# Transposing the values of a linear attention through VectorE squares and device memory

## The chip, the cores and the metric

The kernel runs on one core of a Trainium2 chip. The core has a TensorE (PE in the profile) that multiplies matrices and writes its sums to PSUM, a VectorE (DVE), a ScalarE (ACT), a GpSimd (POOL) and a SyncE (SP), each with an instruction queue of its own that is worked off in order. DMA engines move data between device memory and the on-chip memory SBUF; here SP issues nearly all transfers. The metric is the device time of one execution in microseconds (us), lower is better.

## The reference: what is computed

Two layers of an encoder over 16 learned meta tokens and 256 grid tokens (272 positions, width 2048), in float32. Each layer projects the residual stream `h` once and splits the columns:

```
proj = jnp.einsum('bld,dp->blp', h, w_in)
gq, gk, gv, gr, glr, nq, nk, nv = jnp.split(proj, points, axis=-1)
y_gla = _gla_mixer(gq, gk, gv, gr, glr, gla_w_up, gla_b_up, gla_norm_w)
y_na = _na_mixer(nq, nk, nv, na_rel_bias)
mix = jnp.einsum('blm,md->bld', jnp.concatenate([y_gla, y_na], axis=-1), w_out)
h = _layer_norm(DEEPNORM_ALPHA * h + mix, ln1_w, ln1_b)
ff = square(relu(h @ w_ff1)) @ w_ff2
h = _layer_norm(DEEPNORM_ALPHA * h + ff, ln2_w, ln2_b)
```

The change touches `gv`, the values of the gated linear attention: 4 heads of 256 columns. In that attention a position's output is a sum over positions of scores times values, `einsum('bhts,bhse->bhte', scores, vi)`, so the values are needed with positions as rows. The neighbourhood attention (`_na_mixer`) and the squared-ReLU MLP fill the rest of the layer.

## The kernel before

**Layout.** Activations lie transposed: features on the 128 partitions, positions along the free axis. `x` is 16 tiles of 128 x 272. Every float32 operand is held as two parts, a rounded high part and the rest (`split`, L337-339: an ACT copy and a DVE subtract), and a product is three matmuls: high by high, low by high, high by low.

**Weights.** `weights` and `made` (L180-198) stream the weights in pieces of 128 x 1024 (512 KB): SP loads `raw` (L194), ACT rounds it to `wh` (L217), DVE subtracts to `wl` (L218). Each of the three has three buffers. So a piece's `wh` can be written once PE is done with the piece three before it, and PE then has two more pieces to work on before it needs the new one. A full piece is 24 matmuls of 272 columns (`eight`, L252); where 256 columns are wanted, it is 8 of 512 and 8 of 256.

**Order of the work.** `by_m` walks over output tiles of 128 columns (two pieces each) and calls `pump` between pieces. `pump` takes steps from two queues of Python generators, `fg` and `bg`, which hold the side work: the decay gates (`gates`, L452), the transposes of the values (`v_rows`, L508), the attention heads. A `yield True` marks that the next step contains PE work, and pump spaces such steps. The code is then ordered per engine by a scheduler; what each engine runs is a fixed list.

**The place of the change.** Early in each layer the values are projected, tile by tile, each evicted by `ev_v` (L501): ACT copies the 128 x 272 sum from PSUM to `ft` (L503). Two tiles make one head, and `v_rows` turns a head's two tiles: six TensorE transposes against an identity matrix (L516) into two PSUM banks, then per tile a `split` (L518) of the 256 grid positions into `V` and `vlow` (tiles named `y`), and a `stack` (L519) of the 16 meta positions into `VS`: two ACT copies (L344) and a DVE subtract (L345). `V`, `vlow` and `VS` are read much later, by L715-719 in `gla_head`.

Around it, `gates` multiplies all `x` tiles by a thin matrix (L468), copies the result (`lrt`, L473), builds `lr`, and per head issues two small matmuls (L486), then on ACT two absolute values (L487), an exponential (L488), a logarithm (L489) and a last exponential (`dec`, L492), with a DVE step (L491) between. The next pieces' `wh` copies stand in the same ACT queue.

Of the kernel before, what the change touches and what calls it, by code (L numbers as in the profile page):

```python
# [7 lines left out]
F32 = mybir.dt.float32  # L8
# [6 lines left out]
P = 128  # L15
D = 2048
DC = D // P
T = 256
NM = 16
L = T + NM  # L20
DEPTH = 2
ROWS, GW = 4, 64
GH, GDK, GDV = 4, 128, 256
# [14 lines left out]
MEET = 2  # L38
PAD = 40
PITCH = 288  # L40
WIDE = 1280
HIGHS = {"once": (0, P, 2 * P), "two": (0, P, 2 * P), "all": (0, P, 2 * P), "all2": (0, P, 2 * P), "own2": (0, P + 48, 2 * P + 64)}
LOWS = {"once": (16, P + 32, 2 * P + 64), "two": (16, P + 16, 2 * P + 64), "all": (0, P + 16, 2 * P + 64),
# [15 lines left out]
class Trunk:  # L59
    def __init__(self, ctx, tc, ins, out):  # L60
        self.ctx, self.tc, self.nc = ctx, tc, tc.nc
        self.i, self.out = ins, out
        self.bg, self.fg, self.credit, self.fcredit = deque(), deque(), 0, 0
        self.wants, self.due, self.late, self.low = {}, None, 0, True
        self.x = [None] * DC
        self.stream, self.ready = self.order(), deque()
        pool = lambda name, **k: ctx.enter_context(tc.tile_pool(name=name, **k))
        self.cp = pool("const", bufs=1)
        self.xp = pool("xhl", bufs=1)
        self.yp = pool("yhl", bufs=1)  # L70
        self.wp = pool("wst", bufs=3)
        self.jp = pool("jn", bufs=1)
        self.pm = pool("pm", bufs=4, space=PSUM)
        self.pb = pool("pb", bufs=4, space=PSUM)

    def bank(self):
        return self.pb.tile([P, 512], F32, name="bg", tag="bg")
# [108 lines left out]
    def made(self, ap, ends, kind):  # L186
# [3 lines left out]
        raw = self.wp.tile([P, WB], F32, name="raw", tag="raw")  # L190
        wh, wl = (self.wp.tile([P, WIDE], F32R, name=nm, tag=nm) for nm in ("wh", "wl"))
        wh, wl = self.blocks(wh, *HIGHS[kind]), self.blocks(wl, *LOWS[kind])
# [154 lines left out]
    def pair(self, pool, name, c):  # L347
        both = pool.tile([P, 2, PITCH], F32R, name=f"{name}{c}", tag=f"{name}{c}", bufs=1)
        return Pair(both, dense=name in ("y", "u") and not self.full)


    def layer(self, l):
        nc, tc = self.nc, self.tc
        self.l = l
        self.full = l + 1 < DEPTH
        self.n = n = L if self.full else T
        with ExitStack() as actx:
            pool = lambda name, side, ctx=actx, bufs=1: ctx.enter_context(
                tc.tile_pool(name=name, bufs=bufs, side=side, reuse_waits="tile"))
            a = pool("att", "left")  # L360
            t = lambda nm, s: a.tile(s, F32, name=nm, tag=nm)
            self.qk = [t(f"qk{h}", [P, 2, L]) for h in range(GH)]
            for h in range(GH) if l else ():
                nc.gpsimd.memset(self.qk[h][:, 1, T:], 0.0)
            self.decay = [t(f"dec{h}", [P, 2, L]) for h in range(GH)]
            self.V = a.tile([P, 2 * GH, 2, P], F32R, name="V", tag="V")
            self.vlow = [self.pair(self.yp, "y", 12 + h).both.rearrange("p a c -> p (a c)") for h in range(GH)]
            self.VS = a.tile([80, GH * GDV], F32R, name="VS", tag="VS")
            nc.gpsimd.memset(self.VS.bitcast(F32), 0.0)
            self.y, self.gate, self.done, self.vt = [None] * DC, {}, set(), []  # L370
            if l:
                self.load_gates()
                self.by_m(self.x, [L + 2] * 4, lambda m, ps: self.fixed(self.ev_k, m, ps), pump=(1, NORMS[0]),
                          renew=True)
                first = self.by_k(self.x, L, self.normed)
                self.drain()
                self.lctx.close()
            with ExitStack() as ectx:
                self.ep = pool("early", "right", ectx)
                self.fcredit = 0  # L380
                self.fg.append(self.gates())
                if l == 0:
                    with ExitStack() as xctx:
                        self.xr = pool("xr", "right", xctx)
                        first = self.by_k(self.x, L, self.load_x, wide=True)
                    for m in range(4):
                        self.ev_k(m, first.pop(0)[0])
                for m, ps in enumerate(first):
                    self.ev_v(m, ps[0])
                self.credit, self.alone = 0, True  # L390
                self.by_m(self.x, [L] * 4, lambda m, ps: self.ev_v(4 + m, ps), pump=(1, 1, True))
                self.by_m(self.x, [n] * 4, self.ev_q, pump=(1, 1, True))
                self.drain()
            self.a2 = pool("na", "left", bufs=2)
            with ExitStack() as gctx:
                self.credit = 0
                self.g2 = pool("gla", "right", gctx, 2)
                for h in range(GH):
                    self.bg.append(self.gla_head(h))
                for g in range(2):  # L400
                    self.by_m(self.x, [n] * 4, lambda m, ps: self.ev_r(4 * g + m, ps), pump=(1, GLA_R))
                self.na_tiles()
                for g in range(6):
                    if g == 5:
                        while self.bg:
                            self.step(self.bg, 1)
                        gctx.close()
                        self.ln_open()
                    ns = [n if (4 * g + m) % 3 == 0 else L for m in range(4)]
                    self.by_m(self.x, ns, lambda m, ps: self.ev_na(4 * g + m, ps), pump=(1, GLA_NA, True))  # L410
            self.alone = False
            ps = self.by_k(self.y, n, self.mixed)
            self.drain()
        self.tail(ps)
# [29 lines left out]
    def load_gates(self):  # L444

        place = lambda c: self.yp.tile([P, 2, PITCH], F32, name=f"gw{c}", tag=f"y{c}", bufs=1).rearrange("p a c -> p (a c)")[:, :512]
        *self.wup, self.wlr = (place(c) for c in (8, 9, 10))
# [51 lines left out]
        self.nc.scalar.activation(self.qk[m][:, 0, :], ps, AF.Identity, **how)  # L499

    def ev_v(self, c, ps):  # L501
        vt = self.ep.tile([P, L], F32, name="ft", tag="ft", bufs=4)
        self.nc.scalar.copy(vt, ps)  # L503
        self.vt.append(vt)
        if c % 2:
            (self.fg if c > 3 else self.bg).append(self.v_rows(c // 2, self.vt[-2:]))

    def v_rows(self, h, vt):  # L508

        nc = self.nc  # L510
        yield True
        pt = self.spare(2)
        for i in range(3):
            n = P if i < 2 else NM
            for e in range(2):
                nc.tensor.transpose(pt[e][:n, i * P:i * P + P], vt[e][:, i * P:i * P + n], self.ident)  # L516
        for e in range(2):
            self.split(pt[e][:, :T], self.V[:, 2 * h + e].rearrange("p i c -> p (i c)"), self.vlow[h][:, e * T:e * T + T])  # L518
            self.stack(pt[e][:NM, T:T + P], self.VS[:, h * GDV + e * P:h * GDV + e * P + P], NM, (0, 32), 64)  # L519
            yield  # L520

    def ev_na(self, j, ps):
# [504 lines left out]
    def reuse(self, name, c, dtype):  # L1027

        t = self.xp.tile([P, 2, PITCH], dtype, name=f"{name}{c}", tag=f"x{c}", bufs=1)
        return t.rearrange("p a c -> p (a c)")[:, :512]  # L1030
# [237 lines left out]
```

## Time and profile before

| what | value |
|---|---|
| median of 3 runs | 2325.73 us (2324.75 to 2325.81) |
| the profiled execution | 2325.9 us, of which the span from first to last instruction is 2324.1 us |
| PE / ACT / DVE / POOL busy | 2311.4 / 1230.7 / 1527.8 / 130.1 us |
| granted TensorE clock, mean | 0.999 |
| weight pieces | 770 groups of `wh` copies (805.0 us of ACT) and as many `wl` subtracts (937.8 us of DVE) |
| transposes of values (L516) | 48 matmuls, from 62.8 us to 1283.6 us |

The busy share is an average over the span. A row of a timeline gives start, length, engine, line, operation, tiles and count; in square brackets stands how long the engine was idle before it and what ended that. A matmul's length is longer than its distance to the next one, since matmuls are pipelined, so what a piece costs is read from the starts. ACT's rows also overlap by about 0.1 us.

### The profile page before, as it was taken

Reading aid. Unit: us, or ns where it says so; the run is one execution under the profiler, and the core shown is the slowest. Engines: PE = TensorE matmul, PEld = TensorE weight load, DVE = VectorE, ACT = ScalarE, POOL = GpSimd, SP = SyncE. Lnnn points to the kernel's source line nnn. Section 1 sums busy time; section 2 is a strip of 40 time slices with the busy share of each in tenths; the row PEclk is TensorE's granted clock in tenths of the full one; section 3 lists DMA queues with packets and bytes.
Section 4 is the critical chain, followed back from the end, with each engine's and each line's share of the span. In section 5 each row is a group of like instructions: output and inputs, shape, how many; then the busy total and the mean of one; then the engine's idle time right before and its main releaser. Section 6 shows DMA issues by size and latency. Waiting matters only on the chain.

```text
span 2324.1 us, 45342 instructions
## 1 busy us (share of the span) xinstructions
PE 2311.4 (99%) x18516; PEld 2197.5 (95%) x18516; DVE 1527.8 (66%) x2440; ACT 1230.7 (53%) x2128; POOL 130.1 (6%) x200
## 2 busy tenths in 40 slices
PE   9999999999999999999999999999999999999999
PEld 9999999999999999999999899989988888888888
DVE  5588777775544455547576788878866545666655
ACT  5666765564433344444456767655655334555443
POOL 0021110110000000000020021100100000000000
PEclk9999999999999999999999999999999999999999
DMA  8455545555555555555655555555666666667664
GB/s 265 154 164 153 155 149 167 173 181 181 181 179 178 180 181 182 179 179 178 182 183 166 175 170 160 155 172 181 197 193 193 192 196 192 191 198 221 191 195 150
DMA packets 118304, 419.07 MB, mean 180 GB/s; under 512 B 13512, under 2 KB 14024, under 8 KB 118096
## 3 DMA queue, kind: packets, MB, share of 16 engines
q1 hardware_dynamic: 117808, 415.65, 57.9%
q8 instruction: 145, 2.38, 0.4%
q14 instruction: 63, 0.52, 0.1%
q10 hardware_dynamic: 288, 0.52, 0.1%
HBM read 414.03 MB, written 2.10 MB: 179 GB/s over the span
## 4 chain that ended last, share of the span: by engine, by line
PE 96%; DVE 2%; ACT 1%; issue 1%; DMA 0%; POOL 0%; DVEq 0%; ACTq 0%; SPq 0%; POOLq 0%
PE mm L252 56%; PE mm L264 30%; PE mm L303 4%; PE mm L313 2%; PE bg L303 1%; DVE wl L218 1%; PE bg L837 0%; PE bg L627 0%; PE bg L468 0%; PE mm L775 0%; ACT wh L217 0%; DVE acc L1071 0%; PE mm L801 0%; PE bg L969 0%; PE mm L516 0%
## 5 line engine op out<-in xcount | busy, mean ns | idle before, releaser
L218 DVE TENSOR_TENSOR wl<-raw,wh 128x1024 fp32r<-128x1024 f32 (+1 forms) x770 | 937.8, 1225 | 633.9 <-ACT wh L217 531.5
L217 ACT CAST wh<-raw 128x1024 fp32r<-128x1024 f32 (+1 forms) x770 | 805.0, 1047 | 764.5 <-PE mm L252 344.3
L252 PE MATMUL mm<-x,wh 128*128 128x272 f32 (+3 forms) x4544 | 805.8, 294 | 0.0
L252 PEld LDWEIGHTS mm<-x,wh 128*128 128x128 f32 x4544 | 646.9, 188 | 15.7 <-issue 0.8
L252 PE MATMUL mm<-x,wl 128*128 128x272 f32 (+3 forms) x2432 | 519.8, 284 | 0.0
L252 PEld LDWEIGHTS mm<-x,wl 128*128 128x128 f32 x2432 | 390.7, 188 | 0.0
L252 PE MATMUL mm<-y,wh 128*128 128x272 f32 (+1 forms) x1440 | 235.0, 285 | 0.0
L252 PEld LDWEIGHTS mm<-y,wh 128*128 128x128 f32 x1440 | 199.8, 188 | 0.1
L264 PE MATMUL mm<-x,wh 128*128 128x512 f32 x832 | 193.8, 390 | 0.0
L264 PEld LDWEIGHTS mm<-x,wh 128*128 128x128 f32 x832 | 154.3, 188 | 31.0
L252 PE MATMUL mm<-u,wh 128*128 128x272 f32 (+1 forms) x1056 | 172.1, 285 | 0.0
L264 PE MATMUL mm<-y,wh 128*128 128x512 f32 x688 | 162.3, 389 | 0.0
L264 PEld LDWEIGHTS mm<-y,wh 128*128 128x128 f32 x688 | 128.6, 188 | 26.9 <-issue 0.4
L252 PE MATMUL mm<-y,wl 128*128 128x272 f32 (+1 forms) x720 | 146.4, 284 | 0.0
L252 PEld LDWEIGHTS mm<-u,wh 128*128 128x128 f32 x1056 | 146.3, 188 | 0.0
L264 PE MATMUL mm<-u,wh 128*128 128x512 f32 x496 | 118.2, 390 | 0.0
L252 PEld LDWEIGHTS mm<-y,wl 128*128 128x128 f32 x720 | 112.6, 188 | 0.0
L264 PEld LDWEIGHTS mm<-u,wh 128*128 128x128 f32 x496 | 90.9, 188 | 17.6
L252 PE MATMUL mm<-u,wl 128*128 128x272 f32 (+1 forms) x528 | 107.3, 284 | 0.0
L264 PEld LDWEIGHTS mm<-x,wl 128*128 128x128 f32 x832 | 98.4, 188 | 2.0
L264 PE MATMUL mm<-x,wl 128*128 128x256 f32 x832 | 98.8, 276 | 0.0
L264 PEld LDWEIGHTS mm<-y,wl 128*128 128x128 f32 x688 | 84.3, 188 | 2.8
(288 smaller groups left out, 2301.6 us busy)
## 6 DMA issues: line engine op xcount, KB each, us to landing
raw<-in_wff SPq DMA_DIRECT2D x512, 512.0 KB, 3.6
raw<-in_win SPq DMA_DIRECT2D x190, 512.0 KB, 3.8
raw<-in_wout SPq DMA_DIRECT2D x64, 512.0 KB, 3.7
nb<-in_nab SPq DMA_DIRECT2D x16, 352.0 KB, 4.3
xraw<-in_xT SPq DMA_DIRECT2D x7, 272.0 KB, 5.7
out<-out SPq DMA_DIRECT2D x5, 256.0 KB, 3.0
brow<-in_norm SPq DMA_DIRECT2D x4, 256.0 KB, 4.8
gw<-in_wup SPq DMA_DIRECT2D x4, 196.0 KB
```

Of the source, the lines that this page charges most:

```text
L217: self.nc.scalar.copy(h, r)
L218: self.wl = self.nc.vector.tensor_tensor(lo, r, h.bitcast(F32), ALU.subtract).ins
L252: mm(o, lhsT=self.block(w, j), rhs=rhs, start=first and not i, stop=last and i == len(TURNS[once]) - 1)
L264: self.nc.tensor.matmul(o, lhsT=self.block(both[j // 8][low], j % 8), rhs=rhs, start=first and not i + j, stop=bool(last and i and j == 15 ...
L303: self.nc.tensor.matmul(ps[g + m][:, :n], lhsT=self.block(parts[p][0], 4 * j + m if first else 2 * m + j), rhs=acts[k + j][parts[p][1]][:, ...
L313: self.nc.tensor.matmul(o, lhsT=self.block(both[low], i), rhs=rhs, start=not low and k + i % 2 == 0, stop=k == DC - 2 and i % 2 == 1 and n ...
```

## The change

`ev_v` now pads each 128 x 272 tile with 16 zero columns (a GpSimd memset) to 288, and DVE transposes it in 32 x 32 squares into half of a tile `vt`; each square is turned in place, so the four 32-row bands of a tile still have to be brought side by side. `v_rows` does that with transfers on ACT's queue: it writes a head's `vt` (128 x 576) to a buffer in device memory, `vhop`, and reads it back in nine pieces, eight of 32 partitions x 4 x 64 into `vr` and one of 16 x 4 x 64 into `vm`. `split` and `stack` then read those from SBUF. The TensorE transposes and their two PSUM banks go; the generator has four steps in place of three, and the first is not marked as PE work. Per head that is two DVE transposes, two memsets and ten DMAs more and six matmuls less, eight times in the program.

```diff
+        self.hp = pool("hop", bufs=2, space=bass.MemoryType.DRAM)
...
     def ev_v(self, c, ps):
-        vt = self.ep.tile([P, L], F32, name="ft", tag="ft", bufs=4)
-        self.nc.scalar.copy(vt, ps)
-        self.vt.append(vt)
-        if c % 2:
-            (self.fg if c > 3 else self.bg).append(self.v_rows(c // 2, self.vt[-2:]))
+        h, e = divmod(c, 2)
+        vt = self.ep.tile([P, VR * 32], F32, name="ft", tag="ft", bufs=2)
+        if not e:
+            self.vt = self.ep.tile([P, VR, 2, 32], F32, name="vt", tag="vt", bufs=3)
+        self.nc.scalar.copy(vt[:, :L], ps)
+        self.nc.gpsimd.memset(vt[:, L:], 0.0)
+        self.nc.vector.transpose(self.vt[:, :, e, :], vt)
+        if e:
+            (self.fg if c > 3 else self.bg).append(self.v_rows(h, self.vt))
...
     def v_rows(self, h, vt):
-        nc = self.nc
-        yield True
-        pt = self.spare(2)
-        for i in range(3):
-            n = P if i < 2 else NM
-            for e in range(2):
-                nc.tensor.transpose(pt[e][:n, i * P:i * P + P], vt[e][:, i * P:i * P + n], self.ident)
+        nc, e = self.nc, self.ep
+        hop = self.hp.tile([P, VR, 64], F32, name="vhop", tag="vhop")
+        nc.scalar.dma_start(hop, vt.rearrange("p j e c -> p j (e c)"))
+        yield
+        rows, meta = e.tile([P, 2, 4, 64], F32, name="vr", tag="vr", bufs=2), e.tile([NM, 4, 64], F32, name="vm", tag="vm", bufs=2)
+        at = hop.rearrange("(a k) j c -> k j a c", a=4)
+        for j in range(VR - 1):
+            nc.scalar.dma_start(rows[j % 4 * 32:j % 4 * 32 + 32, j // 4], at[:, j])
+        nc.scalar.dma_start(meta, at[:NM, VR - 1])
+        yield
         for e in range(2):
-            self.split(pt[e][:, :T], ...)
-            self.stack(pt[e][:NM, T:T + P], ...)
+            src = rows[:, :, :, 32 * e:32 * e + 32]
+            self.split(src, ...)
+            self.stack(meta[:, :, 32 * e:32 * e + 32], ...)
             yield
```

In the lists below a row gives the line, the operation, output and inputs with their numbers, and the shape; `x5` is five in a row. Lines of the changed kernel are two later up to `gates` and twelve later from `silu` on, so L219 is the `wh` copy and L220 the `wl` subtract.

**PE, first layer, behind the gates' thin matmuls (`ws`).** Before, head 0's six transposes stand ahead of the next piece:

```order
L468 MATMUL bg_802<-x15_623,ws_765 64x272
L516 MATMUL mm_849<-ident_635,ft_726 128x128
L516 MATMUL mm_850<-ident_635,ft_728 128x128
L516 MATMUL mm_849<-ident_635,ft_726 128x128
L516 MATMUL mm_850<-ident_635,ft_728 128x128
L516 MATMUL mm_849<-ident_635,ft_726 16x128
L516 MATMUL mm_850<-ident_635,ft_728 16x128
L252 MATMUL mm_862<-x0_130,wh_769 128x272 x2
```

After, the piece follows the thin matmuls at once:

```order
L470 MATMUL bg_819<-x15_625,ws_777 64x272
L254 MATMUL mm_877<-x0_132,wh_783 128x272 x2
L254 MATMUL mm_877<-x1_133,wh_783 128x272 x2
L254 MATMUL mm_877<-x0_132,wl_784 128x272
L254 MATMUL mm_877<-x1_133,wl_784 128x272
```

The same is so at the other seven heads; nothing takes the transposes' place on PE.

**ACT, first layer, from the copies of the first values to the gates' `lrt`.** Before, three pieces are rounded there (769, 864, 911):

```order
L503 COPY ft_730<-bg_107 128x272
L217 CAST wh_769<-raw_768 128x1024
L503 COPY ft_732<-bg_108 128x272
L217 CAST wh_864<-raw_863 128x1024
L217 CAST wh_911<-raw_910 128x1024
L473 COPY lrt_835<-bg_802 32x272
```

After, one (783) is; heads 0 and 1 are sent off, and head 0's read-back waits for its write to land:

```order
L518 DMA vhop_780<-vt_729 128x576
L508 COPY ft_742<-bg_110 128x272
L219 CAST wh_783<-raw_782 128x1024
L518 DMA vhop_1019<-vt_738 128x576
L523 DMA vr_866<-vhop_780 32x4x64 x5
L508 COPY ft_812<-mm_746 128x272
L523 DMA vr_866<-vhop_780 32x4x64 x3
L524 DMA vm_867<-vhop_780 16x4x64
L475 COPY lrt_852<-bg_819 32x272
L219 CAST wh_879<-raw_878 128x1024
```

The second and third pieces (879, 926, which answer to 864 and 911) have moved behind `lrt`.

**ACT, first layer, the gates of heads 1 to 3 (`gt`, `dec`).** Before, piece 1061 is rounded ahead of them:

```order
L217 CAST wh_1061<-raw_1060 128x1024
L492 ACTIVATE dec1_85<-gt_944 128x544
L488 ACTIVATE gt_987<-gt_987 128x544
L338 CAST V_88<-mm_997 128x256
L489 ACTIVATE gt_987<-gt_987,one_659 128x544
L344 CAST VS_93<-mm_997 16x128 x2
L503 COPY ft_1040<-mm_954 128x272
```

After, the piece that answers to it, 1081, comes behind all of them and behind head 1's read-back, of which this is the end:

```order
L489 ACTIVATE gt_1058<-bg_1056 128x272
L489 ACTIVATE gt_1058<-bg_1057 128x272
L523 DMA vr_1068<-vhop_1019 32x4x64
L494 ACTIVATE dec2_88<-gt_1009 128x544
L490 ACTIVATE gt_1058<-gt_1058 128x544
L523 DMA vr_1068<-vhop_1019 32x4x64
L491 ACTIVATE gt_1058<-gt_1058,one_661 128x544
L523 DMA vr_1068<-vhop_1019 32x4x64 x2
L494 ACTIVATE dec3_89<-gt_1058 128x544
L523 DMA vr_1068<-vhop_1019 32x4x64 x3
L524 DMA vm_1069<-vhop_1019 16x4x64
L219 CAST wh_1081<-raw_1080 128x1024
```

Between the copies of piece 1022 and piece 1081 there now stand the gates of heads 1, 2 and 3 and nine DMAs, and no piece.

More of the change, by code (lines that the diff above doesn't have):

```diff
@@ L40 @@
 PITCH = 288
+VR = 9
 WIDE = 1280
@@ L369, in layer @@
             nc.gpsimd.memset(self.VS.bitcast(F32), 0.0)
-            self.y, self.gate, self.done, self.vt = [None] * DC, {}, set(), []
+            self.y, self.gate, self.done = [None] * DC, {}, set()
             if l:
@@ L501, in ev_v @@
     def ev_v(self, c, ps):
-        vt = self.ep.tile([P, L], F32, name="ft", tag="ft", bufs=4)
-        self.nc.scalar.copy(vt, ps)
-        self.vt.append(vt)
-        if c % 2:
-            (self.fg if c > 3 else self.bg).append(self.v_rows(c // 2, self.vt[-2:]))
-    def v_rows(self, h, vt):
-        nc = self.nc
-        yield True
-        pt = self.spare(2)
-        for i in range(3):
-            n = P if i < 2 else NM
-            for e in range(2):
-                nc.tensor.transpose(pt[e][:n, i * P:i * P + P], vt[e][:, i * P:i * P + n], self.ident)
-        for e in range(2):
-            self.split(pt[e][:, :T], self.V[:, 2 * h + e].rearrange("p i c -> p (i c)"), self.vlow[h][:, e * T:e * T + T])
-            self.stack(pt[e][:NM, T:T + P], self.VS[:, h * GDV + e * P:h * GDV + e * P + P], NM, (0, 32), 64)
+        h, e = divmod(c, 2)
[7 more added lines that the diff above has]
+            (self.fg if c > 3 else self.bg).append(self.v_rows(h, self.vt))
+    def v_rows(self, h, vt):
+        nc, e = self.nc, self.ep
[8 more added lines that the diff above has]
+        yield
+        for e in range(2):
+            src = rows[:, :, :, 32 * e:32 * e + 32]
+            four = lambda a: a.rearrange("p (i a c) -> p i a c", i=2, a=4)
+            self.split(src, four(self.V[:, 2 * h + e].rearrange("p i c -> p (i c)")), four(self.vlow[h][:, e * T:e * T + T]))
+            to = self.VS[:, h * GDV + e * P:h * GDV + e * P + P].rearrange("p (a c) -> p a c", a=4)
+            self.stack(meta[:, :, 32 * e:32 * e + 32], to, NM, (0, 32), 64)
             yield
```

## Prediction

> **What bounds the kernel.** I read the page first, then the chain of waits, the waits, and last the timelines of TensorE and ACT around the transposes.
>
> ```profile
> span 2324.1 us, 45342 instructions
> PE 2311.4 (99%) x18516; PEld 2197.5 (95%) x18516; DVE 1527.8 (66%) x2440; ACT 1230.7 (53%) x2128; POOL 130.1 (6%) x200
> PE 96%; DVE 2%; ACT 1%; issue 1%; DMA 0%; POOL 0%; DVEq 0%; ACTq 0%; SPq 0%; POOLq 0%
> ACT wh L217 <- PE mm L252: 344.3, 209, 2.2
> ```
>
> TensorE is the bound: 99% busy, 96% of the chain. A matmul taken off it is time gained, and a microsecond in which it waits is a microsecond lost. The last row (us in total, times, longest) says that ACT's rounding of weights waits for TensorE, so ACT runs as far ahead as the buffers let it. What the share of 53% hides is the stretch at the change:
>
> ```profile
> 63.00:83.00 20.00, 20.00 (x165) 19.92 (x164) 10.97 (x22) 18.81 (x43) 0.00 (x0) 1.00 0.30 100
> ```
>
> In this table of windows the columns are length, then PE, weight loads, DVE, ACT, POOL, clock, DMA share, GB/s. Behind the gates' matmuls ACT is busy for 18.81 of 20 us while TensorE waits for nothing. Whatever is added to ACT's queue there has little slack to go into.
>
> **What goes: the transposes.** The timeline of TensorE:
>
> ```profile
> 53.04 0.65 PE L252 MATMUL mm<-x,wh 128*128 128x272 f32 x4
> 55.97 0.65 PE L252 MATMUL mm<-x,wh 128*128 128x272 f32 x4
> 58.91 4.15 PE L468 MATMUL bg<-x,ws 128*64 128x272 f32 x32
> 62.89 0.82 PE L516 MATMUL mm<-ident,ft 128*128 128x128 f32 x6
> 63.47 0.75 PE L252 MATMUL mm<-x,wh 128*128 128x272 f32 x4
> 64.30 0.67 PE L252 MATMUL mm<-x,wh 128*128 128x272 f32 x4
> 65.07 0.66 PE L252 MATMUL mm<-x,wh 128*128 128x272 f32 x4
> 65.81 0.65 PE L252 MATMUL mm<-x,wh 128*128 128x272 f32 x4
> 66.55 0.41 PE L486 MATMUL bg<-lr,up 98*128 98x272 f32 x2
> 66.80 0.67 PE L252 MATMUL mm<-x,wh 128*128 128x272 f32 x4
> ```
>
> By the starts six transposes take 63.47 - 62.89 = 0.58 us. A piece is 55.97 - 53.04 = 2.93 us, so a quarter of it 0.73; the two quarters behind the transposes take 0.83 and 0.77, which is 0.14 more. That makes about 0.7 for a head, and 8 heads give 5.5 us back (at worst 8 x 0.58 = 4.6).
>
> **What is added, beside TensorE.** Rows of the nearest kind:
>
> ```profile
> L339 DVE TENSOR_TENSOR y<-ft,y x64: 411/428/445, 454.6 to 2050.4; 128x272 fp32r<-128x272 f32 x32, 128x256 fp32r<-128x256 f32 x32
> L1169 ACTq DMA_DIRECT2D out<-out x2: 338/366/395, 2317.4 to 2318.7; - x2
> 37.17 0.44 SPq L94 DMA_DIRECT2D qmask<-in_qmask  x1
> out<-out ACTq DMA_DIRECT2D x2, 256.0 KB, 3.7
> vec<-in_vec SPq DMA_DIRECT2D x1, 66.0 KB, 3.8
> xraw<-in_mask SPq DMA_DIRECT2D x1, 80.0 KB, 3.1
> ```
>
> Two DVE transposes of 288 columns: some 0.43 us each by the first row, on an engine busy for 10.97 of the 20 us; hidden. If that cover went, the `wl` subtract behind them would be late by at most 0.9 us a head. Two memsets of 16 columns on POOL, which does nothing in that window: nothing. Ten transfers a head move under 0.6 MB, with DMA 30% busy: as bandwidth, nothing. The `V` copies and `vlow` subtracts read SBUF in place of PSUM and now wait for the landing; their readers come much later, so only what queues behind that wait on ACT and DVE counts.
>
> Two prices are not shown for this shape. An issue on ACT: the two seen there took 0.34 to 0.40 us; a small one on SP 0.44. From below it could be 0.05, if issuing overlaps the instruction ahead as ACT's rows do among themselves. I take 0.35, since a row of the same queue shows it. The trip: writing a head is 295 KB, nearest to the 256 KB at 3.7; a read-back is 32 KB in 128 runs of 256 bytes, nearest to `vec` (128 partitions, two rows of 264 bytes each) at 3.8 and `mask` at 3.1, but half the bytes; I take 3.0, from 2 to 5.
>
> [...]
>
> **What is moved: the roundings.** This carries the sum. ACT's timeline of before:
>
> ```profile
> 63.09 0.38 ACT L473 COPY lrt<-bg 32x272 f32<-32x272 f32 x1 [3.18 <-PE bg L468]
> 68.16 1.23 DVE L218 TENSOR_TENSOR wl<-raw,wh 128x1024 fp32r<-128x1024 f32 x1 [0.79 <-ACT wh L217]
> 72.71 0.66 ACT L488 ACTIVATE gt<-gt 128x544 f32<-128x544 f32 x1
> 74.61 1.05 ACT L217 CAST wh<-raw 128x1024 fp32r<-128x1024 f32 x1
> 75.55 0.66 ACT L492 ACTIVATE dec<-gt 128x544 f32<-128x544 f32 x1
> 76.66 0.36 ACT L338 CAST V<-mm 128x256 fp32r<-128x256 f32 x1
> 77.56 0.51 ACT L344 CAST VS<-mm 16x128 fp32r<-16x128 f32 x2
> 81.47 1.05 ACT L217 CAST wh<-raw 128x1024 fp32r<-128x1024 f32 x1
> 82.42 0.66 ACT L492 ACTIVATE dec<-gt 128x544 f32<-128x544 f32 x1
> 82.99 1.98 ACT L217 CAST wh<-raw 128x1024 fp32r<-128x1024 f32 x2
> ```
>
> `lrt` starts at about 63.09 in both kernels, since the thin matmuls end at 62.89 in both. Before, three later pieces were rounded by then; after, two of these have slid behind `lrt`. From `lrt` to the end of the rounding at 74.61 are 75.66 - 63.09 = 12.57 us of before. The new list up to the end of piece 1022 is that, less 0.7 idle, less a `ft` copy and the exponential, logarithm and pair of absolute values that now come later (2.4), plus one more rounding (1.0): 10.5, so 1022 is ready at 73.6.
>
> From there to piece 1081: before's stretch from 75.55 to 81.47 (5.92), less two `V` (0.5) and four `VS` (1.04) that have moved, plus the gate work of 72.71 to 74.61 (1.90), plus one `dec` (82.99 - 82.42 = 0.57), is 6.85. Nine issues (eight `vr`, one `vm`) at 0.35 add 3.15, the rounding 1.05: 1081 is ready at 84.7. TensorE has five pieces behind the thin matmuls (783, 879, 926, 978, 1022) and four pairs of small gate matmuls (66.80 - 66.55 = 0.25): 62.89 + 5 x 2.93 + 4 x 0.25 = 78.5. It waits 6.2 us. Then `wl`, 1.23 behind `wh`, is late as well, since the matmuls that want `wh` alone run out in 0.4: 0.8 more.
>
> The stalls behind it, by the same two lists:
> - Head 2 is sent off behind 1081 (85.1) and lands at 88.8. Eight issues of `vr`, one of `vm` (3.15) and a `ft` copy, two `VS` and the rounding (0.27 + 0.54 + 1.05) make piece 1169 ready at 93.8. TensorE, having started 1081 at 84.7 + 0.8, wants it 5.9 later, at 91.4: 2.4 + 0.8.
> - Head 3's read-back stands one piece behind its write; its `wl` comes 0.7 late.
>
> That is 10.9 in the first layer. The second:
>
> ```profile
> 1254.04 0.82 PE L516 MATMUL mm<-ident,ft 128*128 128x128 f32 x6
> 1254.24 0.38 ACT L473 COPY lrt<-bg 32x272 f32<-32x272 f32 x1 [3.18 <-PE bg L468]
> 1268.38 1.03 ACT L217 CAST wh<-raw 128x1024 fp32r<-128x1024 f32 x1
> ```
>
> Before's list from `lrt` to the end of that rounding is 15.17 us. After, up to piece 15775, it lacks 0.5 idle, four `V` (1.0), six `VS` (1.6) and a `ft` (0.3), and has a logarithm and a `dec` more (1.2) and nine issues (3.15): 16.1, so 1270.4. TensorE's four pieces and four pairs end at 1254.04 + 11.7 + 1.0 + 0.2 = 1266.9: 3.5 + 0.8. Carried on, piece 15822 costs 0.4 + 0.9, and the pieces behind the read-backs of heads 2 and 3 cost 2.1 + 0.9 and 1.8 + 0.9. Together 11.3.
>
> **The sum.** -5.5 + 10.9 + 11.3 = +16.7. The profiled execution took 2325.9 us, 0.2 above the median, so about 2342. What could make TensorE late next, if these stalls were not there, is nothing that I see: the next such lists hold no DMAs.
>
> **Rivals.**
> 1. *Issues are cheap.* If ACT hands a transfer off in 0.05 us, 8 x 10 issues lose 0.3 each. The first stall falls to 3.5, the second layer's to 0.8, and those behind landings by half: the stalls sum to about 8, so +2 to +4, 2328 to 2330. The SP rows speak for 0.33 or more; nothing speaks for less but that no issue in ACT's mid-stream is in the trace.
> 2. *The trip is slow.* Runs of 256 bytes, eight transfers at once, the raw pieces' own traffic in the same engines: landings 1.5 us later each. Six waits stand behind landings (head 2 and 3 of each layer, write and read-back), and head 1 of each has cover: 6 x 1.5 = 9 more, 2351; with 0.42 for an issue 3 more, and 2354. `vec` at 3.8 speaks for it.
> 3. *The clock falls.* The first stall of 6 us would leave TensorE idle longer than anything in the stretch above.
>
> ```profile
> 5.91 1.11 PE L303 MATMUL mm<-x,wh 128*128 128x272 f32 x4
> 7.27 0.72 PE L303 MATMUL mm<-x,wh 128*128 128x272 f32 x4
> 8.08 0.66 PE L303 MATMUL mm<-x,wh 128*128 128x272 f32 x4
> 4.00:7.00 3.00, 3.00 (x15) 3.00 (x14) 2.45 (x7) 2.32 (x7) 0.00 (x0) 1.00 1.02 355
> ```
>
> Right after TensorE's start six matmuls took 7.27 - 5.91 = 1.36 us in place of 0.81 for the next six, although the clock's column reads 1.00. If each of the two long stalls brings back two such groups, at 1.36 in place of 0.73, that costs 1.3 a time, +2.6: 2345. [...]
> 4. *The other side: everything is covered.* If ACT reached piece 1081 before 78.5, only the -5.5 stayed: 2320.4. That needs ACT's list 6.2 us shorter, and the issues are 3.15 of it; it decides at the point where the issues are free and the gates' steps besides overlap better by 3 us. [...]
>
> **Chances.** The forecast's mechanism, with the stalls at 10 to 36 us over the gain: 0.74 (2331 to 2358; the clock is within it). Cheap issues 0.13, of which half stays within 0.2% (4.65 us, about what a measurement of this kernel can tell from no change). A trip slower still, past 2358, 0.08. All covered 0.05. So slower 0.88, same 0.07, faster 0.05. The range runs from the cheap issues, 2329, to the slow trip with a cold clock, 2354 + 3 and some for the terms beside, 2362.
>
> **What would show it.** Right: TensorE idle for 5 to 7 us at about 78.5 with `wh` from ACT as what ended it, smaller gaps at 88 to 92 and in the second layer at 1267 to 1297, all within the stretches where `vr` is issued; ACT's queue with 0.35 us for an issue; nothing lost elsewhere; no L516. Wrong: gaps elsewhere (raw pieces late because the transfers share queues or semaphores), DVE or POOL as the releaser, or none at all.

## The result, and the profile after

| | median | profiled execution's span |
|---|---|---|
| before | 2325.5 us | 2324.1 us |
| changed | 2349.6 us (2347.7 to 2351.6) | 2347.2 us |

The ratio is 1.0104, 95% interval 1.0092 to 1.0116: slower by 1.0%, 24 us, where 2342 (+16) was forecast. The page of the changed kernel, then its waits of TensorE (us in total, times, longest):

```profile
PE 2318.6 (99%) x18468; PEld 2200.7 (94%) x18468; DVE 1534.9 (65%) x2456; ACT 1233.1 (53%) x2128; POOL 131.8 (6%) x216
PE 92%; DVE 3%; ACT 2%; DMA 1%; issue 1%; ACTq 0%; DVEq 0%; POOL 0%; SPq 0%
```

```profile
PE mm L254 <- ACT wh L219: 9.8, 4, 5.4
PE mm L254 <- DVE wl L220: 4.2, 7, 1.3
PE bg L488 <- DVE lr L347: 1.5, 1, 1.5
```

TensorE's share is still 99% and ACT's still 53%; only the chain shows it, 92% for TensorE in place of 96%. The three rows of waits are new: TensorE now waits 15.5 us in all for the two parts of the weights and for the gates' `lr`. None of the three is in the list of before.

Where that time lies can be read by matching the same rounding in both timelines. Before:

```profile
154.03 1.05 ACT L217 CAST wh<-raw 128x1024 fp32r<-128x1024 f32 x1
1109.69 1.05 ACT L217 CAST wh<-raw 128x1024 fp32r<-128x1024 f32 x1 [1.89 <-PE mm L252]
2278.16 1.05 ACT L217 CAST wh<-raw 128x1024 fp32r<-128x1024 f32 x1 [0.76 <-PE mm L264]
```

After:

```profile
164.31 1.05 ACT L219 CAST wh<-raw 128x1024 fp32r<-128x1024 f32 x1
1119.91 1.05 ACT L219 CAST wh<-raw 128x1024 fp32r<-128x1024 f32 x1 [1.89 <-PE mm L254]
2301.31 1.06 ACT L219 CAST wh<-raw 128x1024 fp32r<-128x1024 f32 x1 [0.76 <-PE mm L266]
```

The lag is 10.3 us behind the first layer's transposes, still 10.2 at 1110 us, and 23.2 near the end. So the first layer loses 10.2 net and the second 13.0, each within the stretch in which the values are turned, and nothing is lost elsewhere. TensorE's timeline around the longest wait and the waits after it:

```profile
78.36 0.65 PE L254 MATMUL mm<-x,wh 128*128 128x272 f32 x4
84.62 1.28 PE L254 MATMUL mm<-x,wh 128*128 128x272 f32 x4 [5.36 <-ACT wh L219]
86.50 1.11 PE L254 MATMUL mm<-x,wh 128*128 128x272 f32 x4
87.86 1.11 PE L254 MATMUL mm<-x,wh 128*128 128x272 f32 x4
94.92 0.76 PE L254 MATMUL mm<-x,wh 128*128 128x272 f32 x4 [1.76 <-ACT wh L219]
1268.91 0.49 PE L488 MATMUL bg<-lr,up 98*128 98x272 f32 x2 [1.51 <-DVE lr L347]
1283.05 0.77 PE L254 MATMUL mm<-x,wh 128*128 128x272 f32 x4 [1.93 <-ACT wh L219]
```

The wait at 79 us is there, and behind it a second loss: six matmuls take 87.86 - 86.50 = 1.36 us in place of 0.73. The windows behind the five waits (columns as in the prediction; the eighth value, ahead of the DMA share, is the granted clock):

```profile
84.00:90.00 6.00, 5.38 (x24) 5.08 (x25) 3.40 (x5) 2.87 (x6) 0.00 (x0) 0.56 0.62 182
95.00:100.00 5.00, 4.50 (x22) 4.29 (x23) 4.81 (x7) 3.57 (x8) 0.00 (x0) 0.66 0.48 144
1270.00:1275.00 5.00, 4.78 (x27) 4.63 (x26) 4.77 (x9) 4.59 (x9) 0.35 (x2) 0.66 0.57 162
1283.00:1288.00 5.00, 4.46 (x22) 4.24 (x23) 3.97 (x7) 4.45 (x10) 0.00 (x0) 0.66 0.49 156
1300.00:1305.00 5.00, 4.21 (x15) 3.64 (x16) 3.71 (x5) 2.71 (x5) 0.00 (x0) 0.66 0.70 210
```

The clock stands at 0.56 to 0.66 there. By these rows 6 x 0.44 + 4 x 5 x 0.34 = 9.4 us go to it, or up to 0.3 less, since the first window begins 0.6 us before its wait ends. The span's balance is then -5.5 (the transposes) + 15.5 (waits) + 9.4 (clock) = 19.4 of 23.1. The remaining 3.7 is not read from a row. Some of it is waiting for `wl` that the rows of waits do not list: the group at 84.62 takes 86.50 - 84.62 = 1.88 us where the next, as slow in clock, takes 1.36, and its first matmul that reads `wl` starts at 85.88, just behind the end of that subtract at 84.60 + 1.23 = 85.83.

### The profile page after: what moved, and what is told of

It is laid out like the page before. It is cut to its first block, busy times and chain, and to the rows that moved or that the text cites. A ratio compares the mean times of both kernels' runs of the same rounds, so it can differ in the third digit from the quotient of the medians.

```text
span 2347.2 us, 45420 instructions
## 1 busy us (share of the span) xinstructions
PE 2318.6 (99%) x18468; PEld 2200.7 (94%) x18468; DVE 1534.9 (65%) x2456; ACT 1233.1 (53%) x2128; POOL 131.8 (6%) x216
## 4 chain that ended last, share of the span: by engine, by line
PE 92%; DVE 3%; ACT 2%; DMA 1%; issue 1%; ACTq 0%; DVEq 0%; POOL 0%; SPq 0%
PE mm L254 53%; PE mm L266 29%; PE mm L305 3%; PE mm L315 2%; DVE wl L220 1%; PE bg L305 1%; ACT wh L219 1%; DMA raw<-in_win 1%; PE bg L849 0%; DMA vr<-vhop 0%; ACTq L523 0%; PE bg L639 0%; PE mm L787 0%; DVE acc L1083 0%; PE mm L813 0%
## 5 line engine op out<-in xcount | busy, mean ns | idle before, releaser
L220 DVE TENSOR_TENSOR wl<-raw,wh 128x1024 fp32r<-128x1024 f32 (+1 forms) x770 | 937.8, 1224 | 638.9 <-ACT wh L219 534.1
L219 ACT CAST wh<-raw 128x1024 fp32r<-128x1024 f32 (+1 forms) x770 | 805.2, 1047 | 760.9 <-PE mm L254 348.3
```

What stands on the lines that cost most here:

```text
L219: self.nc.scalar.copy(h, r)
L220: self.wl = self.nc.vector.tensor_tensor(lo, r, h.bitcast(F32), ALU.subtract).ins
```

## The experiments

Two theories stood after the result. By the first, time is lost in ACT's list: transfers' issues and waits for landings stand ahead of roundings and of `lrt`, and each long wait also costs clock. By the second, the trip itself costs it (traffic, small runs, landings), or the squares on DVE do.

| run | what it is | median, us | ratio to before, 95% |
|---|---|---|---|
| e1 | before, no transposes | 2319.8 | 0.9979 (0.9970 to 0.9989) |
| e5 | changed, squares but no trip | 2320.6 | 0.9980 (0.9971 to 0.9989) |
| e2 | changed, transfers on SP | 2337.7 | 1.0050 (1.0034 to 1.0067) |
| e3 | changed, transfers on GpSimd | 2332.7 | 1.0033 (1.0024 to 1.0043) |
| e6 | six transfers a head, ACT | 2335.7 | 1.0044 (1.0030 to 1.0058) |
| e8 | six, SP, later copies | 2336.3 | 1.0048 (1.0033 to 1.0064) |
| e7 | six, GpSimd, later copies | 2323.4 | 0.9991 (0.9982 to 0.9999) |
| e9 | changed, all heads behind the gates | 2342.6 | 1.0067 (1.0052 to 1.0083) |
| e10 | changed, later copies | 2346.7 | 1.0089 (1.0076 to 1.0103) |
| e11 | six, GpSimd, behind the gates | 2334.5 | 1.0036 (1.0023 to 1.0048) |
| e4 | before, 7 roundings repeated 6 to 14 times | 2392.9, one run | none taken |
| e12 | before, 25 roundings repeated 4 or 5 times | 2428.0, one run | none taken |

### e1 and e5: the gain, and the squares by themselves

```diff
 # e1, in before
-        yield True
-        pt = self.spare(2)
-        for i in range(3):
-...
+        yield
+        pt = vt
...
-            self.stack(pt[e][:NM, T:T + P], ...)
+            self.stack(pt[e][:NM, :P], ...)
```

> The kernel before without the 48 transposes: V and VS are taken straight from the copied tiles, so the values stay unturned (the turning is left out, and nothing is put in its place). The forecast's gain term says 8 x 0.7 = 5.5 us: about 2320. If what follows a transpose on TensorE was slow for another reason, the gain is 8 x 0.58 = 4.6 or less. If moving the steps about is enough to make TensorE wait, this kernel is no faster than before.

2319.8: 5.5 us less than the 2325.3 beside it, the forecast's gain. That it fits to the tenth is partly chance: in e1's profiled execution a wait of TensorE that before has as well, 1.6 us at some 236 us, is followed by a granted clock of 0.66 over 236 to 241 us, and its span is 4.7 us shorter than before's; in e5's the same wait costs no clock, and the span is 6.5 us shorter.

```diff
 # e5, in the changed kernel
...
-        nc.scalar.dma_start(hop, vt.rearrange("p j e c -> p j (e c)"))
-...
+        rows = vt[:, :8].rearrange("p (i a) e c -> p i a (e c)", i=2)
+        meta = vt[:NM, :4].rearrange("p a e c -> p a (e c)")
...
```

> The changed kernel without the trip: memsets and DVE's 32x32 transposes stay, and V and VS are taken from the transposed squares as they lie (the regrouping of the bands is left out, so the values stand in the wrong rows). If DVE's and POOL's added work is hidden, as forecast, this is e1 over again, 2319 to 2321. If the 16 DVE transposes delay wl, up to 0.9 us a head come on top, to 2327.

2320.6, the same as e1 within the intervals. Memsets and DVE transposes are hidden. What takes this gain back and costs 24 us more is the trip and what it does to the lists: the changed kernel is 29 us slower than e5.

### e2 and e3: the transfers on another queue

```diff
-        nc.scalar.dma_start(...)
+        nc.sync.dma_start(...)      # e2; nc.gpsimd in e3; all ten of a head
```

> The changed kernel with the ten transfers of a head on SP's queue in place of ACT's; nothing else is edited. Theory (ACT's queue: issues and what waits in them hold up the roundings, and each long wait brings a stretch of slow TensorE): ACT has no issue to make and four roundings stand ahead of lrt, so the stalls at 79 and 93 us and their slow stretches go; 2320 to 2326. Rival (the trip itself is too slow wherever it is issued, and now SP's loads of weights queue behind the wait for the write's landing, 3.8 us, and nine issues, 3.1 us): about 7 us of delay for a raw piece at every head against some 6 us of lead; 2330 to 2360, with raw landings as what ends TensorE's or ACT's waits.

> The changed kernel with the ten transfers on GpSimd's queue. Theory (ACT's queue): as with SP, but no load of weights stands behind them, so 2319 to 2324, the transposes' gain kept nearly whole. Rival (landings and traffic of 256-byte runs): the V copies on ACT still wait for landings with roundings behind them, so stalls of 1 to 3 us at three or four places stay, 2328 to 2340. Second rival: issuing on GpSimd is slow (1 us each or more), then V is late and the same stalls show with vr as the releaser.

Both are faster than the changed kernel, by 12 and 17 us, and both miss the theory's number. The stall at 79 us is gone in both; others have come. In e2, rows of ACT:

```profile
95.15 1.05 ACT L219 CAST wh<-raw 128x1024 fp32r<-128x1024 f32 x1 [3.64 <-DMA raw<-in_win]
103.71 0.40 ACT L498 ACTIVATE qk<-mm 128x272 f32<-128x272 f32 x1 [3.72 <-PE mm L254]
```

One is the rival's: a raw piece that came late. The other is neither's: the copy of `qk`, which has to wait for TensorE, stands in ACT's list ahead of two roundings, and TensorE waits 1.4 us behind it. In e3, of ACT and then of TensorE:

```profile
1258.24 0.71 ACT L340 CAST V<-vr 128x256 fp32r<-128x256 f32 x2 [4.68 <-DMA vr<-vhop]
1261.20 0.38 ACT L475 COPY lrt<-bg 32x272 f32<-32x272 f32 x1
```

```profile
1263.10 0.49 PE L488 MATMUL bg<-lr,up 98*128 98x272 f32 x2 [3.42 <-DVE lr L347]
```

ACT sits 4.7 us in front of `V`, whose read-back has not landed, with `lrt` behind it; the gates' matmuls, and with them TensorE, wait 3.4 us. That is a second cause beside the issues: a copy that waits for a landing holds up what stands behind it. The changed kernel has the same in small, at 1268.91.

### e6, e7, e8: six transfers, and later copies

```diff
-        hop = self.hp.tile([P, VR, 64], F32, name="vhop", tag="vhop")
-        nc.scalar.dma_start(hop, vt.rearrange("p j e c -> p j (e c)"))
+        hop = self.hp.tile([VR * 32, 4, 64], F32, name="vhop", tag="vhop")
+        at = hop.rearrange("(j k) a c -> k j a c", k=32)
+        for a in range(4):
+            nc.scalar.dma_start(at[:, :, a], vt[32 * a:32 * a + 32].rearrange("p j e c -> p j (e c)"))
...
-        for j in range(VR - 1):
-            nc.scalar.dma_start(rows[j % 4 * 32:j % 4 * 32 + 32, j // 4], at[:, j])
-        nc.scalar.dma_start(meta, at[:NM, VR - 1])
+        nc.scalar.dma_start(rows, hop[:T].rearrange("(i p) a c -> p i a c", p=P))
+        nc.scalar.dma_start(meta, hop[T:L])
...
-        yield
+        for _ in range(3):       # e7 and e8 only, on gpsimd and on sync
+            yield
```

> The changed kernel with the same trip on ACT's queue in six transfers a head in place of ten: four writes of 32 partitions that put each band in its place in device memory, then one read of 128 x 2 x 256 and one of 16 x 256. Theory (what counts is how much of ACT's list stands ahead of a rounding): four issues fewer, 1.2 to 1.4 us a head, and two roundings ahead of lrt in place of one: the stall at 79 us falls from 5.4 to about 1, the next to under 1, and most slow stretches with them; 2327 to 2336. Rival (the landings, not the issues, hold ACT up): write and read-back land no sooner, so 2340 to 2350.

2335.7: at the upper end of the theory's span, 14 us less than the changed kernel. The wait at 79 us became one of 1.7 us at 76.

> Six transfers a head as in e6, but on GpSimd's queue, and two more pump steps between the read-back and the copies that wait for it. Theory (two causes: issues on ACT's queue, as in the changed kernel, and waits for landings ahead of lrt and of roundings, as in e3 at 1263 and 105 us): both go; what is left is the transposes' gain, 2319 to 2322. Rival (something in the trip itself costs time, such as raw pieces landing at 4.1 us in place of 3.8): 2325 or more, with raw as the releaser.

2323.4, 26 us faster than the changed kernel and 0.1% faster than before, the interval just clear of none. Its runs spread from 2320.8 to 2327.9, so the median misses the forecast span of 2319 to 2322 by 1.4. In the profiled execution (span 2319.2) TensorE works through both stretches:

```profile
62.00:130.00 68.00, 68.00 (x615) 67.42 (x613) 47.71 (x80) 48.51 (x97) 16.94 (x30) 1.00 0.64 188
1255.00:1350.00 95.00, 93.73 (x779) 83.60 (x778) 78.26 (x130) 73.10 (x153) 18.53 (x36) 1.00 0.60 182
```

PE is busy for all 68 us, at clock 1.00, with the whole trip in place. So the trip need not hold TensorE up. The median is still 2.8 us above that of e5, which makes no trip; whether the trip costs that is open. The granted clock does not explain the spread: it is 0.999 in the run of 2327.9 and in that of 2320.8.

> The same as e7 on SP's queue. Theory (in e2 the loads of weights queued behind SP's waits for the landing of the write and for the tiles): fewer issues and longer pauses cut that, but the wait for the write's landing, about 4 us, still stands ahead of raw loads: 2322 to 2332, with raw as what ends ACT's idle time ahead of the stalls. If SP's queue was not the cause in e2 but the waits of V were, this equals e7.

2336.3, slower than the theory's span. Rows of ACT and of TensorE:

```profile
87.26 0.40 ACT L498 ACTIVATE qk<-mm 128x272 f32<-128x272 f32 x1 [3.80 <-PE mm L254]
```

```profile
90.49 1.27 PE L254 MATMUL mm<-x,wh 128*128 128x272 f32 x4 [2.42 <-ACT wh L219]
```

As in e2, `qk` waits for TensorE, with two `V`, four `VS` and the roundings behind it in ACT's list, and 2.4 us later TensorE waits for them. The queue was not what the expectation made of it: a raw load is what ends ACT's idle time only once near it (1.6 us at 95.8).

### e9, e10, e11: the place of the steps

```diff
 # e9 (and e11, with e7's transfers and without its later copies)
-            self.vt = self.ep.tile([P, VR, 2, 32], F32, name="vt", tag="vt", bufs=3)
+            self.vt = self.ep.tile([P, VR, 2, 32], F32, name="vt", tag="vt", bufs=4)
...
-            (self.fg if c > 3 else self.bg).append(self.v_rows(h, self.vt))
+            self.fg.append(self.v_rows(h, self.vt))
 # e10
         nc.scalar.dma_start(meta, at[:NM, VR - 1])
-        yield
+        for _ in range(3):
+            yield
```

> The changed kernel with all four heads' steps queued behind the gates in the foreground queue, where the first two heads ran beside them in the background queue (and vt with four buffers in place of three). The same ten transfers a head on ACT's queue, the same trip; only their place in ACT's list differs: between 63 and 85 us no read-back of head 1 stands among the gates, and a rounding follows every gate. Theory (what counts is the place of the issues among gates and roundings, not that ACT issues 80 transfers): the stall of 5.4 us at 79 goes, what is left are waits of 1 to 2 us behind landings: 2324 to 2334. Rival (80 issues at 0.35 to 0.5 us on ACT are too many wherever they stand): 2340 to 2350.

> The changed kernel with two more pump steps between a head's read-back and the copies of V that wait for it; the transfers and their queue are as in the changed kernel. If the waits of V for landings carry the loss, it falls to 2330 or below. If the issues ahead of the roundings carry it, head 1's and head 2's eighteen issues now stand together behind the gates (6 to 8 us of ACT in one piece), and it stays at 2340 to 2355.

e9's wait at 79 us is gone, as expected, but its time is 2342.6, a miss by 9 us. Rows of TensorE in e9:

```profile
116.08 1.28 PE L254 MATMUL mm<-x,wh 128*128 128x272 f32 x4 [5.06 <-ACT wh L219]
1312.57 0.80 PE L254 MATMUL mm<-x,wh 128*128 128x512 f32 x1 [6.02 <-ACT wh L219]
```

The read-backs of heads 2 and 3 now stand together in ACT's list, and between 102.26 and 114.98 us no rounding starts; fifteen issues stand there, some behind a wait for a landing, and ACT idles for 9.4 us in all. e10, at 2346.7 on the second branch of its expectation, has this for heads 1 and 2, as its expectation said (rows of ACT):

```profile
79.91 1.03 ACT L219 CAST wh<-raw 128x1024 fp32r<-128x1024 f32 x1
81.64 3.45 ACTq L523 DMA_DIRECT2D vr<-vhop  x7
86.81 3.82 ACTq L523 DMA_DIRECT2D vr<-vhop  x8
91.16 2.94 ACT L219 CAST wh<-raw 128x1024 fp32r<-128x1024 f32 x3 [9.14 <-DMA vr<-vhop]
```

Ten microseconds lie between two roundings, and TensorE waits 7.25 us for the one at 91.16. In these two kernels the longest waits stand where the most issues stand between two roundings: seventeen ahead of the one at 92 (e10), fifteen and eighteen ahead of those at 116 and 1312 (e9). The changed kernel does not fit so well: nine stand ahead of its wait of 5.4 us and nine ahead of the next, of 1.8. Each of these runs also changes the order of ACT's list; none keeps the changed kernel's order and takes the issues alone out of it, so how the loss divides between issues and roundings that have moved behind other work is not shown by a run.

> Six transfers a head on GpSimd's queue as in e7, without the added pump steps, but with all heads behind the gates as in e9. Theory: neither issues on ACT nor waits of V ahead of lrt in the first layer: 2320 to 2324, like e7. If it is slower than e7, the waits of V for the read-back are what is left.

2334.5, 11 us slower than e7: a miss, on the branch that the expectation named last. The waits are again behind `V` copies that wait for their landing (ACT idle for 7.3 us ahead of 104.2 and for 3.7 ahead of 1300.7, TensorE for 1.2 and 3.7).

### e4 and e12: what a wait costs in clock

```diff
 # e4 and e12, in before
+DELAYS = {180: 6, 200: 7, ...}      # number of the piece: repeats
...
             nc.sync.dma_start(raw[:, c], ap[:, c])
+            for _ in range(DELAYS.get(self.made_n, 0)):
+                h = self.pairs(wh, slice(c.start // P, c.stop // P))
+                self.tc.keep_in_program_order(nc.scalar.copy(h, ...))
```

> The kernel before, with the rounding of seven pieces in the first layer's MLP repeated 6, 7, 8, 9, 10, 12 and 14 times ahead of the real one (the output is unchanged), so that TensorE waits for wh by growing lengths. A repeat takes about 0.95 us and the lead is about 4.8 us, so the waits are expected at roughly 1, 2, 3, 4, 5, 7 and 9 us. Forecast's rival 3 (only long waits cost clock): the three or four longest are followed by a slow stretch of 1.3 to 2.5 us, the short ones by none. Theory after the result (any wait of TensorE beyond about 1.5 us is followed by half-speed matmuls, about 2.5 us of loss, whatever its length): nearly all seven. If the slow stretches of the changed kernel come from something else there (transfers, PSUM), none is slow here.

> As e4, but 25 pieces of the first layer with 4 or 5 repeats of the rounding by turns: waits of TensorE of about 1 and 2 us (in e4 six repeats gave 3.0 us). If a slow stretch follows every wait, whatever its length, all 25 sites show groups of six matmuls at 1.36 us; if it depends on length and on when the wait falls, as e2 (1.2 us: slow, 1.4 us: not) and e3 (3.4 us: not) hint, some of the 2 us sites do and hardly any of the 1 us sites.

e4's waits came out at 3.0 to 12.5 us, and the clock falls behind all seven, to between 0.50 and 0.66 over five us. The first and the last, windows of eight us from the wait's end:

```profile
595.00:603.00 8.00, 8.00 (x52) 7.70 (x52) 4.25 (x4) 1.84 (x3) 0.00 (x0) 0.79 0.62 199
1009.00:1017.00 8.00, 7.99 (x42) 7.91 (x43) 4.65 (x4) 1.05 (x1) 0.00 (x0) 0.63 0.60 197
```

e12's waits did not come out at the 1 and 2 us that were expected but at 0.4 to 6.4 us. Behind waits of 0.5 + 0.5, 1.6 + 0.5, again 1.6 + 0.5, and 3.6 us (windows of five and six us, the last of eight):

```profile
534.00:540.00 6.00, 5.00 (x39) 4.76 (x39) 4.20 (x5) 2.74 (x5) 0.00 (x0) 1.00 0.44 117
747.00:752.00 5.00, 4.04 (x30) 3.83 (x31) 3.93 (x4) 0.41 (x1) 0.00 (x0) 1.00 0.42 113
1115.00:1120.00 5.00, 4.51 (x23) 4.29 (x23) 3.25 (x3) 0.00 (x0) 0.00 (x0) 0.66 0.59 183
1147.50:1155.50 8.00, 7.97 (x39) 7.67 (x40) 6.43 (x12) 2.29 (x3) 0.00 (x0) 0.60 0.56 162
```

Here a wait of 1 us costs no clock (1.00 from 534 to 540 us). One of 2 us does at three of five places in e12, 0.66, 0.70 and 0.72 against 1.00 at the other two (the second and third rows are the same wait without and with it), and the 1.6 us at 236 to 250 us, which every kernel has, do in e1, e3 and e10 alone. Behind the eight waits of 3.6 to 6.4 us in e12 the clock falls each time: the first four matmuls take 1.27 to 1.28 us, where they take 0.77 behind the wait of 1 us at 534.56. The 3.4 us wait of e3 at 1263.10 was followed by no slow matmul (clock 1.00 from 1263 to 1268 us). The price does not follow the wait's length: in those eight us 8 x 0.21 = 1.7 us behind 3.0, 8 x 0.40 = 3.2 behind 3.6, and 8 x 0.37 = 3.0 behind 12.5; the least is 1.6, behind a wait of 5.3 us in e12. So e4's and e12's added roundings, without any transfer, bring the slow stretches that the changed kernel shows. What makes the same wait cost clock at one place and not at another is shown by no run. Waits of 1.6 to 2.1 us are among those that cost clock, where the prediction's rival 3 expected it of the two long stalls alone.

## Why the prediction was right, point by point

- **What bounds the kernel, and the gain.** Right: 5.5 us were forecast, e1's median shows 5.5.
- **DVE, POOL and bandwidth at nothing.** Right: e5 for the two engines, and e7 for the bandwidth, up to the 2.8 us left open there.
- **The first stall.** Right in place and releaser, and near in size; that its sum came out to a tenth is luck. Piece 1081 was forecast ready at 84.7; rows of ACT after:

```profile
72.29 1.06 ACT L219 CAST wh<-raw 128x1024 fp32r<-128x1024 f32 x1
80.03 0.75 ACT L491 ACTIVATE gt<-gt,one 128x544 f32<-128x544 f32 x1
80.03 0.79 ACTq L523 DMA_DIRECT2D vr<-vhop  x2
81.69 0.66 ACT L494 ACTIVATE dec<-gt 128x544 f32<-128x544 f32 x1 [0.92 <-DVE gt L493]
81.71 1.28 ACTq L523 DMA_DIRECT2D vr<-vhop  x3
83.04 0.44 ACTq L524 DMA_DIRECT2D vm<-vhop  x1
83.52 1.04 ACT L219 CAST wh<-raw 128x1024 fp32r<-128x1024 f32 x1 [1.18 <-DMA vr<-vhop]
93.83 1.04 ACT L219 CAST wh<-raw 128x1024 fp32r<-128x1024 f32 x1
```

  It was ready at 83.52 + 1.04 = 84.56, and 1022 at 73.35 where 73.6 was forecast. TensorE waits 5.4 where 6.2 was forecast. But the sum charged all nine issues to ACT, 3.15 us. The rows show issues running while ACT works (80.03, twice, and 81.69 with 81.71): five of the nine ran under ACT's work or its waits, and the last four held it up for 1.2 us. In their place ACT waited 1.9 us for DVE ahead of three `dec` (0.9 of it at 81.69), which the sum does not have: with the roundings moved away, too little stands between a head's logarithm (L491) and its `dec` to cover DVE's step between them. So at this stall the rounding's place behind three heads' gates weighs more than the issues: without the 1.2 us TensorE would still wait some 4 us (an estimate, 5.4 - 1.2).
- **The price of an issue and of the trip.**

```profile
L523 ACTq DMA_DIRECT2D vr<-vhop x64: 309/442/807, 57.4 to 1308.3; - x64
DMA to landing us min/median/max: 1.7/2.8/5.6
vhop<-vt ACTq DMA_DIRECT2D x8, 288.0 KB, 3.8
```

  An issue took 0.44 us in the median where 0.35 was taken, just above the upper bound of 0.42, though ACT loses it only where it has no other work under way; the read-back landed after 2.8 (3.0 taken) and the write after 3.8 (3.7).
- **The stalls behind it.** Mis-sized. Piece 1169 was forecast ready at 93.8 and was at 94.9, but TensorE, slowed, wanted it at 93, so it waited 1.8 + 0.5 in place of 2.4 + 0.8. There the issues do count: of the rows ahead of 93.83, the last six issues leave ACT idle for 2.5 us. All stalls together were summed at 22.2; the rows show 15.5.
- **The second layer's start of `lrt`.** Wrong. It was taken at once behind the thin matmuls. Rows of ACT:

```profile
1263.72 0.41 ACT L340 CAST V<-vr 128x256 fp32r<-128x256 f32 x1 [0.36 <-DMA vr<-vhop]
1264.03 1.05 ACT L219 CAST wh<-raw 128x1024 fp32r<-128x1024 f32 x1
1266.03 0.38 ACT L475 COPY lrt<-bg 32x272 f32<-32x272 f32 x1
```

  A `V` that waited for its landing, a rounding and more stood ahead of it. Ahead of these, the write's landing and the issues behind it had left ACT idle for 5.7 and 1.5 us. So the gates' matmuls waited 1.5 us, a stall that the sum does not have; the next, for piece 15775, was 1.9 + 0.5 in place of 3.5 + 0.8. The prediction named the waits of `V` and counted only the roundings behind them.
- **The clock (rival 3).** This is the term that was mis-sized most. It was given two long stalls at 1.3 us, +2.6, and left out of the sum; measured are five stretches and 9.4 us. Two errors went into it: the slow stretch was sized by the start of the kernel, and only long waits were thought to bring one, where e12 shows it behind some waits of 2 us. The slow clock also ate part of the later stalls, as at piece 1169. So 6.7 us too much in stalls, 9.4 too little in clock and the 3.7 not read from a row make the 6.4 by which the sum of +16.7 falls short of the span's 23.1. That the forecast comes so near owes something to errors that cancel: without the 9.4 us of clock, which its sum does not hold, these rows come to 13.7, below the forecast.
- **Rivals.** Cheap issues: out as a price, by the row of L523, but at the first stall its mechanism, issues that overlap, holds for five of nine, and TensorE waits all the same. All covered: out, but e7 comes within 3 us of it (2323.4 against 2320.4), with no issue in ACT's list and the copies that wait for landings late. Turning the 128 x 128 blocks on TensorE, as before does, is the faster way by the medians (2325.5 against 2349.6); by e7 what turns on that choice is 0.1% either way, and the loss came with ACT's list.

## What to carry to other kernels

Work that is moved off the bounding engine goes into another engine's list, and what counts there is not the busy share (53% before and after) but the longest stretch between two steps that the bounding engine waits for: lay the new list out by the durations of the old one, as for piece 1081, and enter in it waits for landings, waits for other engines that the old order covered, and issues of transfers where the engine has no work under way to cover them. Put transfers that wait on a queue that feeds nothing urgent, with their consumers late: e7, which does both, took 2323.4 us, where the changed kernel took 2349.6. In e4 and e12 a slower clock followed waits of TensorE of some 2 us at three of five places and waits of 3.0 us or more at all fifteen, though e3's of 3.4 us was followed by none; an estimate from these is to price a wait of some 2 us with an even chance, and one above 3 us with near certainty, of 1.6 to 3.2 us lost to the clock on top.

## What was not expected of the hardware

The price in clock of short waits: none at 1 us in e12, present or absent at 1.6 to 3.4, and from 1.6 to 3.2 us however long the wait. And an issue's price went with the transfer, not with the queue, on ACT and SP: a read-back of 32 KB in 128 runs took 0.44 us on ACT's queue and 0.43 on SP's in e2, where SP's loads of 512 KB took 0.33. On ACT's queue it ranged from 0.31 to 0.81 with no size changed, and it can run while ACT is still at work, as the rows at 80.03 show. The row of e2:

```profile
L523 SPq DMA_DIRECT2D vr<-vhop x64: 303/430/577, 56.8 to 1292.9; - x64
```
